# GpSimd takes three of the four products of each early rotary embedding, TensorE sums two more row tiles of the modulation, VectorE's order in the opening is set anew

## The chip, the cores and the metric

One core of a Trainium2 chip runs the whole program. The metric is the time of one execution on the device in microseconds, as the median of several runs; the kernel before takes 719.49 us (three runs, 719.28 to 719.74).

## The reference, cut to what matters

Two layers act on x, 512 rows of 1024 features. Each layer first works out a modulation from a conditioning vector c, then a gain-and-shift of the normalised rows, then a mixer, and adds the gated result to x:

```python
shift, scale, gate = split(silu(c) @ mod_w[i] + mod_b[i], 3)
h = rms_norm(x, norm_g[i]) * (1 + scale) + shift
q, k, v, g = split(h @ w_in)                 # layer 0: retention
q = rope(q, positions) * HK ** -0.5          # x1*cos - x2*sin, x1*sin + x2*cos
k = rope(k, positions)
scores = (q @ k.T) * decay                   # 4 heads, 256 wide
o = layer_norm(scores @ v)
x = x + gate * ((o * silu(g)) @ w_out)
```

Layer 1 is an attention with forget gates over 16 heads; the change does not touch it. Only the opening of layer 0 matters below: the sum over the 1024 rows of `mod_w` that gives shift and scale, the products of h with the weights of q and k, and the rotary embedding (rope) of q and k of the first two heads.

## The kernel before, in words

**Numbers.** Products are made from pairs: an operand is cut into a high part in a short format (`wh`, `act`) and the rest (`wl`, the second `act`), and TensorE adds three products (high by high, high by low, low by high). ScalarE casts the high part, VectorE subtracts it to get the low part: `wl<-raw,wh` (128x1024), `act<-x,act` and `act<-rt,act` (128x512).

**The opening.** x comes in as four row tiles of two halves. ScalarE squares them with a running sum, VectorE makes the reciprocal roots and scales the tiles, TensorE transposes them (`p<-ident,x`), ScalarE copies the result out (`big<-p`). The modulation comes in four groups of 256 columns of shift and of scale, `m0`, `m2`, `m4`, `m6`; a group is eight row tiles of `mod_w`, two in a transfer. `DIRECT` (line 38) says for each group how many of its eight row tiles TensorE sums itself, with the weights as the stationary operand and one column of `csilu` as the moving one (`r<-csilu,raw`, 128x1, four calls a row tile). The other row tiles are summed by VectorE into `macc` (one TENSOR_SCALAR, then SCALAR_TENSOR_TENSOR, each waiting for the one before), and four calls `r<-ones,macc` then sum over the partitions. In the kernel before, `m0` has four direct row tiles, the others none. After a group, VectorE writes `mod_a` and `mod_s`, ScalarE makes two feature tiles of h (`act` and `x`), VectorE the low parts, and TensorE can multiply. The first products fill six banks, `s`: q and k of head 0 and q of head 1, 18 products for each of the eight feature tiles, 144 in all. Where TensorE would have nothing to do before them, the planner puts products that nobody reads, `s<-ones_r` (here called fillers), since in the profile the granted clock of TensorE falls to 0.50 for a stretch behind one with little work.

**The ropes.** ScalarE copies the six banks to SBUF (`kept`, tiles `rt`). The function `rope` then makes four products of 128x512 with cos and sin (tiles `trig`), one difference and one sum; the results are split into high and low parts, which the score products `r<-act,act` of head 0 read. For the three ropes of the opening (q and k of head 0, q of head 1) all operands lie in SBUF; later ropes read PSUM.

**Who sets the order.** Nothing is ordered by hand. Every operation is recorded by `Sched` with a priority; `order` then runs through a model of the five engines with a cost for each operation (`cost`), and writes each engine's queue in the order in which the model started the work. On the chip each engine takes its queue strictly in that order and waits on semaphores. So a change of the model's costs moves instructions on all engines. All recorded operations carry the line of one helper, L448, in the profile. The model's costs that the change touches: a DMA's bytes, GpSimd's time for an element-wise operation, and the doubled cost of a TensorE call in a tick of 3.41 us that follows a tick with little work.

**GpSimd's queue** in this stretch holds, before the change, only DMA issues: four transfers `raw<-in_ret_w_in` that add weights onto weights in SBUF for head 0, and then two more for head 1.

Of the kernel before, what the change touches and what calls it, by code (L numbers as in the profile page):

```python
# [10 lines left out]
ALU = mybir.AluOpType  # L11
# [23 lines left out]

ORD = "m0:2 q0:0 k0:0 m2:2 q1:0 m4:2 q0:1 k0:1 m6:2 q1:1"

DIRECT = (4, 0, 0, 0)

SUMS = -22.0  # L40

# [3 lines left out]

ROPE_AT = 32

LATE_SS = 4

GO = (-20.0, -15.0, -10.0, -5.0)  # L50

LATER = 4.0

LAST = (1, 2, 3)

# [128 lines left out]
class Sched:  # L184
# [7 lines left out]
    def __init__(self, tc, kinds, phys):  # L192
        self.tc, self.kinds, self.phys = tc, kinds, phys
        self.tasks, self.clock, self.off, self.extra = [], 0.0, 0.0, []
        self.made = {k: 0 for k in kinds}
        self.uid = 0
        for attr in self.ENG:
            setattr(self, attr, Proxy(self, attr, getattr(tc.nc, attr)))

# [48 lines left out]
    def cost(self, t, op, args, kw, ins, outs):  # L248

        n = max([v.words() for v in outs], default=0)  # L250
        if op == "dma_start":
            v = (ins + outs)[0]
            t.bytes = 4 * v.words() * (v.part[1] - v.part[0])
            if not outs:
                t.bytes = 4 * ins[0].words() * (ins[0].part[1] - ins[0].part[0])
            if "accum_op" in kw:
                t.bytes *= 4
            return {"POOL": 1.02, "SP": 0.06, "ACT": 0.1}[t.eng]
        if t.eng == "PE":
            if op == "transpose":  # L260
                t.cols = 256
                return 0.109
            m = args[2].words()
            t.cols = m if args[2].dtype == F32R else 4 * m
            if m < 64:
                return 0.213
            return max(0.109, 0.002 + m / 2260.0) if args[2].dtype == F32R else max(0.109, m / 600.0)
        ptr = sum(isinstance(kw.get(k), View) for k in ("scale", "bias", "scalar", "scalar1"))
        if t.eng == "ACT":
            if op == "activation" and args[2] in TABLES:  # L270
                t.table = TABLES[args[2]]
            sb = ins[0].buf.kind not in PSUM_KINDS
            return 0.052 + n / 1200.0 + 0.093 * (ptr + ("accum_out" in kw)) + 0.042 * sb
        if t.eng == "POOL":
            return 0.1 + n / (510.0 if op == "tensor_scalar" else 450.0)
        n = max([n] + [v.words() for v in ins])
        psum = any(v.buf.kind in PSUM_KINDS for v in ins + outs)
        fast = op in ("tensor_scalar", "tensor_copy") and not psum
        return 0.069 + 0.061 * ptr + n / (1920.0 if fast else 960.0)
# [19 lines left out]
    def order(self):  # L299
# [7 lines left out]
        busy = {e: True for e in avail}  # L307
        ev, count, out, table = [(START, 0, -i, e, None) for i, e in enumerate(busy)], 0, [], None
        hw = dma = reach = 0.0
        soft, soft_wait = [], []  # L310
        ticks = {-1: 0}
        left = sum(t.eng == "PE" for t in tasks)
        for t in tasks:
# [17 lines left out]
        while True:  # L331
            moved = True
            while moved:
                moved = False
                for e in avail:
                    if busy[e]:
                        continue
                    held, got = [], None
                    while avail[e]:
                        x = heapq.heappop(avail[e])  # L340
                        if fits(x[2]):
                            got = x[2]
                            break
                        held.append(x)
                    for x in held:
                        heapq.heappush(avail[e], x)
                    if got is None and e == "PE" and now > 1.5 and self.idle is not None and self.idle.buf.slot is not None:

                        got = self.filler()
                    if got is None:  # L350
                        continue
                    moved = True
                    if self.idle is not None and e == "PE" and not got.filler and self.idle.buf in got.bufs:
                        self.idle = None
                    for b in got.new:
                        ph = self.kinds[b.kind][0]
                        b.slot = free[ph].pop(0)
                        used[b.kind] += 1
                        turn[b.kind] += 1
                    out.append(got)  # L360
                    got.start = now
                    if e == "PE":
                        tick = int(now / TICK)
                        if ticks.get(tick - 1, 0) < TICK_COLS:
                            got.cost *= 2.0
                        tick = int((now + got.cost) / TICK)
                        ticks[tick] = ticks.get(tick, 0) + got.cols
                    if e == "PE":
                        left -= not got.filler or got is self.first
                        reach = max(reach, got.prio) if left else now + 1e9  # L370
                    busy[e] = True
                    count += 1
                    end = now + got.cost
                    if got.table not in (None, table):
                        end += 1.3
                        table = got.table
                    heapq.heappush(ev, (end, 0, count, e, None))
                    if got.bytes:
                        if e == "POOL":
                            soft.append(got)  # L380
                            a = end + 0.6
                        else:
                            hw = max(hw, now + 0.05) + 0.45
                            a = hw + 0.6
                        heapq.heappush(ev, (a, 3, count, None, got))
                    else:
                        got.done = end
                        heapq.heappush(ev, (end, 1, count, None, got))
# [3 lines left out]
            while ev and ev[0][0] <= now:  # L392
                _, what, _, e, t = heapq.heappop(ev)
                if what == 0:
                    busy[e] = False
                elif what == 3 and t.eng == "POOL" and t is not soft[0]:

                    soft_wait.append(t)
                elif what == 3:
                    dma = max(now, dma) + t.bytes / 360e3  # L400
                    t.done = dma + 0.5
                    if t.eng == "POOL":
                        t.done = now + t.bytes / 360e3 + 1.4
                    count += 1
                    heapq.heappush(ev, (t.done, 1, count, None, t))
                elif what == 1:
                    if t.bytes and t.eng == "POOL":
                        soft.pop(0)
                        if soft and soft[0] in soft_wait:
                            count += 1  # L410
                            soft_wait.remove(soft[0])
                            heapq.heappush(ev, (now, 3, count, None, soft[0]))
                    for b in t.bufs:
                        b.users -= 1
                        if b.users == 0 and b.kind is not None:
                            free[self.kinds[b.kind][0]].append(b.slot)
                            used[b.kind] -= 1
                    for s in t.next:
                        lat = self.LAT if t.eng != s.eng else 0.0 if t.eng == "PE" else 0.13
                        s.ready = max(s.ready, t.done + lat)  # L420
                        s.wait -= 1
                        if not s.wait:
                            count += 1
                            heapq.heappush(ev, (s.ready, 2, count, None, s))
                else:
                    heapq.heappush(avail[t.eng], (t.prio, t.seq, t))
        if ev or any(avail.values()):
            todo = {e: [(t.emit[1], [(b.kind, b.seq) for b in t.new]) for _, _, t in sorted(avail[e])[:4]]
# [99 lines left out]
def trunk(tc, x, c, positions, mod_w, mod_b, norm_g, ret_w_in, ret_w_out, fox_w_in, fox_b_f,  # L528
# [6 lines left out]
    with ExitStack() as es:  # L535
# [348 lines left out]
        xt = []  # L884
        for t in range(NT):
            xt.append([s.buf("x", 512) for _ in range(2)])
            with s.at(-60.0):
                for hf in range(2):
                    SY.dma_start(xt[t][hf], xs[t * P:(t + 1) * P, hf * 512:hf * 512 + 512])
        with s.at(-60.0):  # L890
            pc = pr_(64)
            T.transpose(pc[:, 0:8], crow, ident[0:8, 0:8])
# [127 lines left out]
        def rope(key, b1, b2):  # L1020
            t1, t3 = (s.buf("rt") for _ in range(2))
            t2, t4 = (s.buf("rt") for _ in range(2)) if b1.buf.kind in PSUM_KINDS else (b1, b2)
            V.tensor_tensor(out=t1, in0=b1, in1=cos, op=ALU.mult)
            V.tensor_tensor(out=t3, in0=b1, in1=sin, op=ALU.mult)
            V.tensor_tensor(out=t2, in0=b2, in1=sin, op=ALU.mult)
            V.tensor_tensor(out=t4, in0=b2, in1=cos, op=ALU.mult)
            res = []
            V.tensor_tensor(out=t1, in0=t1, in1=t2, op=ALU.subtract)
            V.tensor_tensor(out=t3, in0=t3, in1=t4, op=ALU.add)
# [731 lines left out]
```

## Time and profile before

| | |
|---|---|
| median of three runs | 719.49 us (719.28 to 719.74) |
| the profiled execution | 719.05 us |
| its span, first to last instruction | 717.2 us |
| TensorE busy | 700.6 us, 98% of the span |
| VectorE busy | 603.2 us, 84% |
| GpSimd busy | 123.4 us, 17% |
| first product of the layer (`s<-act,wh`) | starts at 23.11 us |
| last stop of TensorE in the opening | ends at 68.86 us |
| first score product (`r<-act,act`) | starts at 95.75 us |

The span is read with the work around it in mind: an execution's time is about 1.9 us above its span. TensorE's busy share counts fillers too, so the opening has to be read in the timeline, not in the share. A group of the profile joins rows of the same tiles; a one-column product of 32-bit operands leaves two records for each call.

### The profile page before, as it was taken

To read this page: it belongs to the slowest core of one execution; us is meant where nothing else is said; L and a number is where in the kernel's file an instruction comes from. 1 tells how busy PE (TensorE), PEld (TensorE's weight loads), DVE (VectorE), ACT (ScalarE), POOL (GpSimd) and SP (SyncE) were. 2 spreads that over 40 slices of the span, in tenths; PEclk is the share of its full clock that TensorE was granted. 3 is DMA by queue.
4 is the path that set the end of the run, shared out by engine and by line. 5 is a ranking of instruction groups with operands and counts; after the bars stand their busy time and mean duration, and the time that the engine had idled before them with its cause. 6 is when DMAs were issued, how large, how long until landed. Compare 5 with 4: busy or idle time off the path is not lost.

```text
span 717.2 us, 10155 instructions
## 1 busy us (share of the span) xinstructions
PE 700.6 (98%) x3362; PEld 575.1 (80%) x3362; DVE 603.2 (84%) x1309; ACT 409.1 (57%) x761; POOL 123.4 (17%) x171
## 2 busy tenths in 40 slices
PE   7999999999999999999999999999999999999995
PEld 6777888888888888888888887788887788888884
DVE  5899999999969786998997979876687977799825
ACT  6558573655355435875524554547667577789512
POOL 1001100200010001002000100054352355531011
PEclk9999999999999999999999999999999999999998
DMA  8993864877666627717668118495655566736202
GB/s 283 349 323 82 186 219 112 175 234 231 129 149 208 198 37 160 273 53 146 204 198 302 74 65 286 146 220 128 162 137 135 126 165 144 177 112 186 82 17 100
DMA packets 79634, 120.34 MB, mean 168 GB/s; under 512 B 7016, under 2 KB 39904, under 8 KB 79584
## 3 DMA queue, kind: packets, MB, share of 16 engines
q1 hardware_dynamic: 66176, 98.71, 42.4%
q0 software_dynamic: 13408, 21.01, 17.1%
q8 instruction: 26, 0.43, 0.3%
q14 instruction: 24, 0.20, 0.1%
HBM read 111.25 MB, written 4.25 MB: 161 GB/s over the span
## 4 chain that ended last, share of the span: by engine, by line
PE 78%; DVE 9%; ACT 2%; issue 2%; DMA 1%; POOL 1%; DVEq 0%; POOLq 0%; ACTq 0%
PE p L448 52%; PE r L448 15%; PE a L448 11%; DVE wl L448 1%; DVE t L448 1%; DVE xn L448 1%; POOL lg L448 1%; ACT lg L448 1%; DVE sx L448 1%; DVE st L448 1%; DVE x L448 1%; DVE tg L448 1%; DMA ck<-in_k_mask 1%; DMA st<-st 0%; ACT st L448 0%
## 5 line engine op out<-in xcount | busy, mean ns | idle before, releaser
L448 DVE TENSOR_TENSOR wl<-raw,wh 128x1024 fp32r<-128x1024 f32 x126 | 153.4, 1222 | 21.9 <-ACT wh L448 11.3
L448 ACT CAST wh<-raw 128x1024 fp32r<-128x1024 f32 x126 | 131.3, 1052 | 68.5 <-PE p L448 41.6
L448 PE MATMUL p<-wh,big 128*128 128x512 f32 x384 | 135.6, 402 | 0.0
L448 PEld LDWEIGHTS p<-wh,big 128*128 128x128 f32 x384 | 71.8, 189 | 13.1
L448 PE MATMUL p<-wh,sf 128*128 128x512 f32 x256 | 80.6, 392 | 0.0
L448 PE MATMUL p<-wl,big 128*128 128x512 f32 x192 | 76.4, 398 | 0.0
L448 POOL DMA_DIRECT2D raw<-in_ret_w_in x16 | 19.4, 1212 | 257.1 <-ACT sf L448 62.4
L448 PE MATMUL p<-wh,act 128*128 128x512 f32 x192 | 62.8, 393 | 0.0
L448 DVE SCALAR_TENSOR_TENSOR macc<-raw,csilu,macc 128x512 f32<-128x512 f32 x80 | 59.6, 746 | 0.6
L448 POOL TENSOR_SCALAR lg<-lg,t 128x512 f32<-128x512 f32 (+1 forms) x64 | 42.6, 712 | 82.4 <-DVE t L448 68.2
L448 PEld LDWEIGHTS p<-wh,sf 128*128 128x128 f32 x256 | 48.0, 188 | 9.6
L448 PE MATMUL p<-act,wh 128*128 128x512 f32 x160 | 53.3, 393 | 0.0
L448 PE MATMUL p<-wl,sf 128*128 128x512 f32 x128 | 50.2, 392 | 0.0
L448 PE MATMUL p<-big,wh 128*128 128x512 f32 x128 | 46.4, 420 | 0.0
L448 PE MATMUL r<-act,sh 128*128 128x512 f32 x120 | 42.7, 391 | 0.1
L448 PEld LDWEIGHTS p<-wh,act 128*128 128x128 f32 x192 | 36.0, 188 | 7.3
L448 PEld LDWEIGHTS p<-wl,big 128*128 128x128 f32 x192 | 36.2, 189 | 6.2
L448 ACT ACTIVATE lg<-lg,t 128x512 f32<-128x512 f32 (+1 forms) x64 | 35.9, 562 | 9.1 <-DVE t L448 8.7
L448 PE MATMUL p<-wh,go 128*128 128x512 f32 x112 | 39.2, 402 | 0.2 <-DVE oa L448 0.2
L448 PE MATMUL p<-wl,act 128*128 128x512 f32 x96 | 37.8, 394 | 0.6 <-DVE wl L448 0.6
L448 POOL DMA_DIRECT2D ck<-in_k_mask x32 | 28.5, 1083 | 52.2 <-DVE t L448 52.2
L448 DVE TENSOR_TENSOR ph<-r,ph 128x128 fp32r<-128x128 f32 (+2 forms) x64 | 30.8, 485 | 6.8 <-ACT ph L448 6.3
(203 smaller groups left out, 1574.4 us busy)
## 6 DMA issues: line engine op xcount, KB each, us to landing
raw<-in_ret_w_in SPq DMA_DIRECT2D x48, 512.0 KB, 4.9
raw<-in_mod_w SPq DMA_DIRECT2D x64, 256.0 KB, 6.0
raw<-in_fox_w_in SPq DMA_DIRECT2D x32, 512.0 KB, 4.5
raw<-in_ret_w_in POOLq DMA_DIRECT2D x16, 512.0 KB, 6.3
raw<-in_mod_w SPq DMA_DIRECT2D x16, 512.0 KB, 4.7
raw<-in_ret_w_out SPq DMA_DIRECT2D x16, 512.0 KB, 4.8
ck<-cum_dram SPq DMA_DIRECT2D x16, 448.0 KB, 4.3
x<-in_x SPq DMA_DIRECT2D x16, 256.0 KB, 5.5
```

Of the source, the lines that this page charges most:

```text
L448: getattr(eng, op)(*[real(v) for v in args], **{k: real(v) for k, v in kw.items()})
```

## The change

Five edits:

- `DIRECT` goes from (4, 0, 0, 0) to (4, 2, 0, 0): the first two row tiles of `m2` are summed by TensorE. That is eight more one-column calls and one small product that puts the bias into the bank; VectorE sums six row tiles there in place of eight, and the bias is no longer added by it.
- `ROPE_E = "VGGG"`: where a rope's operands lie in SBUF, its first product stays on VectorE and the other three go to GpSimd. Three ropes, nine products.
- The model: GpSimd's element-wise operations are costed at n/340 in place of n/450, the loads of x with 1.45 times their bytes, and calls of 64 columns or fewer are not doubled in a slow tick.
- `LOOK`: in the model's first 30 us, VectorE doesn't start an operation when one of better priority will be ready within 0.2 us.
- The order of every queue in the opening follows from these.

```diff
-DIRECT = (4, 0, 0, 0)
+DIRECT = (4, 2, 0, 0)
+ROPE_E = "VGGG"
+SLOW = 1.45
+LOOK = 30.0
...
+            t.bytes *= self.slow
...
-            return 0.1 + n / (510.0 if op == "tensor_scalar" else 450.0)
+            return 0.1 + n / (510.0 if op == "tensor_scalar" else 340.0)
...
+                    if got is not None and e == "DVE" and now < LOOK and any(
+                            x.prio < got.prio - 1.0 and x.ready < now + 0.2 and fits(x) for x in soon):
+                        heapq.heappush(avail[e], (got.prio, got.seq, got))
+                        continue
...
-                        if ticks.get(tick - 1, 0) < TICK_COLS:
+                        if ticks.get(tick - 1, 0) < TICK_COLS and got.cols > 64:
                             got.cost *= 2.0
...
+            s.slow = SLOW
             with s.at(-60.0):
                 for hf in range(2):
                     SY.dma_start(xt[t][hf], xs[t * P:(t + 1) * P, hf * 512:hf * 512 + 512])
+            s.slow = 1.0
...
-            V.tensor_tensor(out=t1, in0=b1, in1=cos, op=ALU.mult)
-            V.tensor_tensor(out=t3, in0=b1, in1=sin, op=ALU.mult)
-            V.tensor_tensor(out=t2, in0=b2, in1=sin, op=ALU.mult)
-            V.tensor_tensor(out=t4, in0=b2, in1=cos, op=ALU.mult)
+            eng = [V if b1.buf.kind in PSUM_KINDS or c == "V" else G for c in ROPE_E]
+            for e, o, i0, i1 in zip(eng, (t1, t3, t2, t4), (b1, b1, b2, b2), (cos, sin, sin, cos)):
+                e.tensor_tensor(out=o, in0=i0, in1=i1, op=ALU.mult)
```

What this moves, at three places.

**TensorE ahead of the first product of the layer.** `raw_113` and `raw_116` are the direct row tiles of `m0`, `macc` the rest of `m0`, `s_119<-ones_r` the fillers, `s<-act,wh` the first products. Before:

```order
L448 MATMUL p_286<-ident,x_111 128x128 x4
L448 MATMUL r_247<-csilu,raw_113 128x1 x2
L448 MATMUL r_247<-csilu,raw_116 128x1 x8
L448 MATMUL r_247<-ones,macc_278 128x1 x4
L448 MATMUL s_119<-ones_r 128x512 x5
L448 MATMUL s_347<-act_337,wh_309 128x512
```

With the change (`raw_132` is the first transfer of `m2`):

```order
L464 MATMUL p_298<-ident,x_111 128x128 x4
L464 MATMUL r_237<-csilu,raw_116 128x1 x8
L464 MATMUL r_319<-vecs,ident 128x4
L464 MATMUL s_119<-ones_r 128x512 x2
L464 MATMUL r_237<-ones,macc_292 128x1 x4
L464 MATMUL s_119<-ones_r 128x512 x5
L464 MATMUL r_319<-csilu,raw_132 128x1 x2
L464 MATMUL s_119<-ones_r 128x512
L464 MATMUL r_319<-csilu,raw_132 128x1 x6
L464 MATMUL s_368<-act_352,wh_324 128x512
```

The sums of `m2`'s two row tiles and six fillers now stand between `m0`'s last sum and the first product, where five fillers stood. Ahead of the transposes, eleven fillers stand in place of four.

**VectorE and GpSimd at the ropes.** `rt` are rope tiles, `trig` cos and sin, `vr` and the `act` beside it the values of head 0, `wl` low parts of weights. VectorE before, from the first rope product on:

```order
L448 TENSOR_TENSOR rt_884<-rt_670,trig_722 128x512
L448 TENSOR_TENSOR rt_889<-rt_670,trig_705 128x512
L448 TENSOR_TENSOR rt_670<-rt_686,trig_705 128x512
L448 SCALAR_TENSOR_TENSOR act_902<-vr_852,t_880,act_892 128x512
L448 TENSOR_TENSOR wl_906<-raw_675,wh_850 128x1024
L448 TENSOR_TENSOR wl_915<-raw_680,wh_882 128x1024
L448 TENSOR_TENSOR wl_924<-raw_534,wh_899 128x1024
L448 TENSOR_TENSOR wl_933<-raw_548,wh_921 128x1024
L448 TENSOR_TENSOR rt_686<-rt_686,trig_722 128x512
L448 TENSOR_TENSOR rt_884<-rt_884,rt_670 128x512
```

VectorE with the change, from its one product of q's rope to the first difference of k's rope (`rt_976<-rt_976,rt_715`); `big<-p,u` is a gate tile whose first operand lies in PSUM:

```order
L464 TENSOR_TENSOR wl_933<-raw_712,wh_903 128x1024
L464 TENSOR_TENSOR wl_942<-raw_558,wh_921 128x1024
L464 TENSOR_TENSOR wl_952<-raw_582,wh_938 128x1024
L464 TENSOR_TENSOR rt_907<-rt_907,rt_691 128x512
L464 TENSOR_TENSOR rt_912<-rt_912,rt_709 128x512
L464 TENSOR_TENSOR rt_976<-rt_715,trig_754 128x512
L464 TENSOR_TENSOR act_983<-rt_907,act_972 128x512
L464 TENSOR_TENSOR big_989<-p_810,u_931 128x512
L464 TENSOR_TENSOR act_995<-rt_912,act_985 128x512
L464 TENSOR_TENSOR big_989<-p_814,u_946 128x512
L464 TENSOR_TENSOR rt_1004<-rt_725,trig_754 128x512
L464 TENSOR_TENSOR rt_976<-rt_976,rt_715 128x512
```

Ahead of these rows stand the product `rt_907<-rt_691,trig_754`, one `wl` and one `act<-vr,t,act`. GpSimd with the change:

```order
L464 DMA raw_523<-in_ret_w_in 128x2x512
L464 TENSOR_TENSOR rt_912<-rt_691,trig_739 128x512
L464 TENSOR_TENSOR rt_691<-rt_709,trig_739 128x512
L464 TENSOR_TENSOR rt_709<-rt_709,trig_754 128x512
L464 TENSOR_TENSOR rt_978<-rt_715,trig_739 128x512
L464 TENSOR_TENSOR rt_715<-rt_721,trig_739 128x512
L464 TENSOR_TENSOR rt_1008<-rt_725,trig_739 128x512
L464 TENSOR_TENSOR rt_721<-rt_721,trig_754 128x512
L464 TENSOR_TENSOR rt_725<-rt_762,trig_739 128x512
L464 TENSOR_TENSOR rt_762<-rt_762,trig_754 128x512
L464 DMA raw_1042<-in_ret_w_in 128x2x512
```

The nine products stand behind the four transfers of head 0 and ahead of the transfers of head 1; VectorE's difference `rt_907<-rt_907,rt_691` reads what the second of them writes, its sum `rt_912<-rt_912,rt_709` what the first and the third write, and `rt_976<-rt_976,rt_715` what the fifth writes.

**TensorE at the scores of head 0**, with the change. `act_972`, `act_983` are q's first half, `act_1022` and `act_1037` high and low part of k's first half:

```order
L464 MATMUL p_734<-wh_938,sf_171_816 128x512
L464 MATMUL r_1040<-act_972,act_1022 128x512
L464 MATMUL r_1040<-act_983,act_1022 128x512
L464 MATMUL r_1040<-act_972,act_1037 128x512
L464 MATMUL r_1049<-act_972,act_1022 128x384
```

The three halves of the product stand at the same place in TensorE's queue as before the change, some 300 products behind the first of the layer, and ten of them run on k's first half before thirteen products of head 1's k follow.

More of the change, by code (lines that the diff above doesn't have):

```diff
@@ L196, in __init__ @@
         self.uid = 0
+        self.slow = 1.0
         for attr in self.ENG:
@@ L309, in order @@
         hw = dma = reach = 0.0
-        soft, soft_wait = [], []
+        soft, soft_wait, soon = [], [], []
         ticks = {-1: 0}
@@ L424, in order @@
                             heapq.heappush(ev, (s.ready, 2, count, None, s))
-                else:
+                            if s.eng == "DVE":
+                                soon.append(s)
+                else:
+                    if t in soon:
+                        soon.remove(t)
                     heapq.heappush(avail[t.eng], (t.prio, t.seq, t))
```

## The prediction, made before the changed kernel was run

> **What bounds the kernel now.** I read the page's busy times first, then TensorE's waits, then the timeline of the opening.
>
> ```profile
> PE 700.6 (98%) x3362; PEld 575.1 (80%) x3362; DVE 603.2 (84%) x1309; ACT 409.1 (57%) x761; POOL 123.4 (17%) x171
> PE s L448 <- DVE act L448: 0.9, 2, 0.5
> PE s L448 <- ACT act L448: 0.6, 1, 0.6
> PE p L448 <- DVE wl L448: 0.6, 1, 0.6
> ```
>
> TensorE is the bound: 98% busy. Only what makes it stop, or run at the lower clock, moves the end. Of its waits behind the first product of the layer these four matter, 2.1 us together; the timeline places them, and columns are start, length, operation.
>
> ```profile
> 9.45 1.20 PE L448 MATMUL s<-ones_r 128*128 128x512 f32 x4
> 11.50 3.56 PE L448 MATMUL p<-ident,x 128*128 128x128 f32 x16 [0.85 <-ACT x L448]
> ...
> 16.38 1.94 PE L448 MATMUL p<-ident,x 128*128 128x128 f32 x16
> 18.16 2.29 PE L448 MATMUL r<-csilu,raw 128*128 128x1 f32 x20
> 20.31 1.03 PE L448 MATMUL r<-ones,macc 128*128 128x1 f32 x8
> 21.20 2.12 PE L448 MATMUL s<-ones_r 128*128 128x512 f32 x5
> 23.11 1.91 PE L448 MATMUL s<-act,wh 128*128 128x512 f32 x4
> ...
> 34.22 1.66 PE L448 MATMUL s<-act,wh 128*128 128x512 f32 x6 [0.62 <-ACT act L448]
> 36.27 0.50 PE L448 MATMUL s<-act,wh 128*128 128x512 f32 x1 [0.39 <-DVE act L448]
> ...
> 45.50 0.50 PE L448 MATMUL s<-act,wh 128*128 128x512 f32 x1 [0.55 <-DVE act L448]
> ...
> 68.86 0.50 PE L448 MATMUL p<-wl,act 128*128 128x512 f32 x1 [0.58 <-DVE wl L448]
> ```
>
> The four products from 23.11 take 1.91 us, 0.48 each; the six from 34.22 take 1.66, 0.28 each. The windows give the reason: a granted clock of 0.50, there and under the first transposes.
>
> ```profile
> 12.00:14.00 2.00, 2.00 (x11) 2.00 (x10) 1.80 (x15) 1.73 (x4) 0.00 (x0) 0.50 1.10 347
> 22.00:25.00 3.00, 3.00 (x9) 2.32 (x8) 2.88 (x6) 2.64 (x4) 0.00 (x0) 0.50 1.10 354
> ...
> 80.00:95.00 15.00, 15.00 (x68) 12.43 (x67) 14.93 (x22) 7.58 (x11) 1.20 (x1) 1.00 0.98 254
> ```
>
> So the opening loses the 2.1 us of waits and about 1.0 us of half clock (from 23.11 to some 25.0, at half speed): **3.1 us** is all that a better opening can give back. In the last row, TensorE and VectorE are both full from 80 to 95; that is where the ropes lie.
>
> **The opening, worked out.** Taken off VectorE are two of the eight links of `m2`'s chain of sums:
>
> ```profile
> 26.13 3.11 DVE L448 SCALAR_TENSOR_TENSOR macc<-raw,csilu,macc 128x512 f32<-128x512 f32 x4
> 32.36 0.16 DVE L448 TENSOR_TENSOR mod_a<-r,vecs 128x2 f32<-128x2 f32 x1
> ```
>
> A link is 0.67 to 0.79 us, so 1.3 to 1.6, and its order no longer drops other work between them. `m2` is what the waits at 34.22 and 36.27 hang on (`mod_a` is written at 32.36), `m4` the one at 45.50, a group behind on the same engine. All three, 1.6 us, should go.
>
> TensorE pays. Its ten calls at 18.16 take 2.29 us, 0.23 each; eight more are 1.83, the bias product some 0.1. They stand ahead of the first product and so delay it unless TensorE was free. I follow the queue: eleven fillers at 0.25 to 0.30 from 9.45 end near 12.2, and the transposes start 0.7 us later than at 11.50; if the fillers hold the clock up, the first 16 transposes take 1.94 us as the second 16 do, and not 3.56 (1.6 less); two fillers and the bias add 0.6. `m0`'s last sum, which ended at 21.3, ends at 21.3 + 0.7 - 1.6 + 0.6 = 21.0. Then six fillers (1.5) and eight calls (1.8): the first product at 24.3 in place of 23.11, **1.2 us later**. The half clock (1.0) should be gone, since more fillers lie in the stretch. The wait at 68.86 stays (VectorE is 1.3 us earlier, TensorE about as much): say 0.3 of it is left over and above. Sum: 1.6 + 1.0 - 1.2 + 0.2 = 1.6 us gained. Bounds: 3.1 us gained at best; at worst the clock is at 0.50 over the eight calls (1.8 more) and one further stretch of products (3.4 us at half speed, 1.7), 2 us lost. I take **-1.6**.
>
> The remaining edits (costs of x's loads and of GpSimd, small calls, `LOOK`) touch no duration; they act by the order that this sum follows.
>
> **The ropes, worked out.** Off VectorE come nine products of 0.60 us from start to start, 5.4 us in all. On GpSimd the operation exists in the trace only at the end:
>
> ```profile
> 691.66 1.29 POOL L448 TENSOR_TENSOR x<-x,x 128x512 f32<-128x512 f32 x1 [39.81 <-ACT tm L448]
> 696.82 0.75 DVE L448 SCALAR_TENSOR_TENSOR x<-x,t,x 128x512 f32<-128x512 f32 x1
> 697.10 1.61 POOL L448 TENSOR_TENSOR x<-x,x 128x512 f32<-128x512 f32 x1 [4.15 <-ACT tm L448]
> ```
>
> 1.29 us alone, 1.61 where it overlaps the last 0.47 us of a VectorE operation with two inputs in SBUF. Rows from the attention say more:
>
> ```profile
> 497.00 1.89 POOL L448 TENSOR_SCALAR lg<-lg,t 128x256 f32<-128x256 f32 x2 [0.97 <-DVE t L448]
> 497.51 1.23 DVE L448 TENSOR_TENSOR wl<-raw,wh 128x1024 fp32r<-128x1024 f32 x1 [0.60 <-ACT wh L448]
> 507.13 0.83 POOL L448 TENSOR_SCALAR lg<-lg,t 128x256 f32<-128x256 f32 x2 [1.95 <-DVE t L448]
> L448 DVE TENSOR_TENSOR qn<-qn,t x16: 676/684/941, 437.8 to 565.0; 128x512 f32<-128x512 f32 x16
> 558.38 1.78 POOL L448 TENSOR_SCALAR lg<-lg,t 128x256 f32<-128x256 f32 x2 [0.85 <-DVE t L448]
> 558.46 1.54 DVE L448 TENSOR_TENSOR qn<-qn,t 128x512 f32<-128x512 f32 x2
> ```
>
> The same pair of GpSimd operations takes 0.83 us in the clear and 1.89 with one `wl<-raw,wh` of 1.23 beside it: 1.06 more, nearly that operation's whole length. At 558 GpSimd was at work when VectorE began, and VectorE's operation took 0.94 in place of 0.68 (the longest of 16). I read this as one way to SBUF that either holds while the other waits, and VectorE's next operation in line keeps it. [...]
>
> What does VectorE run beside the nine products? Its groups from 79.7 to 98.1 (busy, mean):
>
> ```profile
> L448 DVE TENSOR_TENSOR wl<-raw,wh 128x1024 fp32r<-128x1024 f32 x6 | 7.2, 1222 | 0.0
> L448 DVE TENSOR_TENSOR rt<-rt,trig 128x512 f32<-128x512 f32 x8 | 5.4, 687 | 0.0
> L448 DVE TENSOR_TENSOR act<-rt,act 128x512 fp32r<-128x512 f32 x4 | 2.7, 687 | 0.0
> L448 DVE TENSOR_TENSOR rt<-rt,rt 128x512 f32<-128x512 f32 x4 | 2.6, 686 | 0.0
> L448 DVE SCALAR_TENSOR_TENSOR act<-vr,t,act 128x512 fp32r<-128x512 f32 x2 | 1.5, 748 | 0.0
> L448 DVE TENSOR_TENSOR big<-p,u 128x512 f32<-128x512 f32 x2 | 1.4, 686 | 0.0
> ...
> 80.49 2.01 DVE L448 TENSOR_TENSOR rt<-rt,trig 128x512 f32<-128x512 f32 x3
> 83.08 4.78 DVE L448 TENSOR_TENSOR wl<-raw,wh 128x1024 fp32r<-128x1024 f32 x4
> 97.33 0.69 DVE L448 TENSOR_TENSOR act<-rt,act 128x512 fp32r<-128x512 f32 x1
> 95.75 3.26 PE L448 MATMUL r<-act,act 128*128 128x512 f32 x15
> ```
>
> No idle time, and only `big` reads PSUM: the rest, 19.4 of the 21 us, has two SBUF inputs. Let T0 be the start of VectorE's first rope product (80.49 before; some 1.3 earlier now). With the new order and full lock-out: product 0.60, `act` 0.66 and four `wl` at 1.18 lead to T0+6.0 with nothing done on GpSimd. The first difference needs its second product: T0+8.6. The sum needs the third, T0+9.9, and ends at 10.5. Six operations of 0.60 follow, to 14.1; GpSimd has the 1.2 us of the two `big` for its fourth and fifth product and needs 2.6: k's first difference starts at T0+15.5. It, two sums, a `wl` and the `act` take 3.5: k's low part stands at **T0+19.0**. Without lock-out no wait remains, and it is T0+14.3.
>
> TensorE came to the scores at 95.75, T0+15.3 then. With the opening's 1.6 us gained and VectorE's 1.3, it comes 0.3 nearer, to T0+15.0, and its third score product, 0.5 later, reads k's low part: a wait of 19.0 - 15.5 = 3.5 us. k's second half needs GpSimd's seventh product (two more, 2.6 us, with no free time beside VectorE's row): T0+21.6, and four operations later, T0+24.0, its low part stands; TensorE, released at 19.0, has eight score products (1.3), thirteen others (2.95) and two more before it, and waits 0.3. Together 3.8. Where GpSimd holds the way when VectorE wants it, VectorE waits too: 0.26 in the row of `qn`, at most 1.29 for a product. At three or four such meetings that is 1 to 4 us; I take 1.2, near the row. The rope term: **+5.0**, from 0 (all hidden; there is no gain, since TensorE doesn't stop at the scores now) to 8 (3.8 + 4). The third rope's products end the row on GpSimd and are needed a head later. Behind them on GpSimd's queue stand head 1's transfers, the first of which was issued here before:
>
> ```profile
> 120.85 1.20 POOL L448 DMA_DIRECT2D raw<-in_ret_w_in  x1 [39.51 <-DVE t L448]
> ```
>
> GpSimd had been idle for 39.5 us, so products that end near 106 delay nothing there.
>
> Sum on the profiled execution, 719.05: -1.6 + 5.0 = **+3.4, 722.45**. It lies 0.44 under the median of the runs, 719.49, so for the median I say **722.9**.
>
> **The rivals.**
>
> *Hidden products (faster).* GpSimd's fifth product must be done by about T0+12 for TensorE not to stop; begun at T0 that is 2.4 us a product at most. If the way is shared finely, or VectorE's own waits for casts leave it free often enough, a product takes 1.3 to 2.4 us, and only the opening is left: 719.49 - 1.6 = 717.9, at best 716.4. For it: the 1.61 us with a partial overlap; against it, 1.06 us of lock-out by one `wl`, and a VectorE without a gap. 0.24.
>
> *Half lock-out (the same).* GpSimd slips in at the seams, and VectorE is never held: half of 3.8, 1.9, against 1.6: 719.8. 0.14.
>
> *A cold clock on top (slower).* Eight one-column calls ahead of the first product are little work, as 18.2 to 21.2 was, behind which the clock fell to 0.50 at 22. If the clock is down there again, the opening loses 2 in place of gaining 1.6, and with the ropes the time is 719.49 + 2 + 5 = 726.5. Against it: six fillers now stand among the calls. [...] 0.14.
>
> **How the numbers follow.** My forecast, lock-out with a warm opening, 0.48. An interval of 0.2% is about what a measurement of this kernel can tell from no change, 718.05 to 720.93. Faster: the hidden case's 0.24 less a little, 0.23. The same: 0.15. Slower: forecast and cold clock, 0.62. The range 717.2 to 727.2 takes in the hidden case, the forecast with its bounds (719.5 to 726) and most of the cold one; the forecast's own range is 720.5 to 726.
>
> **What would show it.** GpSimd's rows `rt<-rt,trig` between 78 and 106 us: 2.5 us or more on average is lock-out, 1.3 to 2.0 is not. VectorE idle before `rt<-rt,rt`, put down to GpSimd, and TensorE idle before `r<-act,act` of 3 us or more, put down to VectorE's or ScalarE's `act`. In the opening: no wait at 34, 36 and 45 us, the first product near 24.3 us, a granted clock of 1.00 from 12 to 25. I am wrong if TensorE doesn't stop at the scores, or if the opening itself is slower.

## The result, and the profile after

The changed kernel takes 729.38 us (median of four runs, 728.02 to 729.80), the kernel before 719.62 beside it: a ratio of 1.0133, with a 95% interval of 1.0115 to 1.0150. By that ratio it is 9.6 us slower, where 3.4 had been forecast, and above the range of 717.2 to 727.2. The profiled execution has a span of 726.9 us, against 717.2.

First the page of the changed kernel (busy times) and TensorE's waits (total, times, longest):

```profile
PE 705.9 (97%) x3391; PEld 579.6 (80%) x3391; DVE 606.3 (83%) x1297; ACT 408.8 (56%) x761; POOL 138.3 (19%) x180
PE r L464 <- DVE act L464: 3.4, 1, 3.4
PE r L464 <- ACT act L464: 3.3, 1, 3.3
PE p L464 <- DVE wl L464: 1.7, 3, 0.9
```

Nine products have left VectorE, yet it is busy 3.1 us longer than the 603.2 before. TensorE has two waits of over 3 us, and the timeline puts both at the scores of head 0:

```profile
24.44 1.40 PE L464 MATMUL s<-act,wh 128*128 128x512 f32 x5
...
83.85 0.50 PE L464 MATMUL p<-wl,sf 128*128 128x512 f32 x1 [0.57 <-DVE wl L464]
...
87.78 0.50 PE L464 MATMUL p<-wl,sf 128*128 128x512 f32 x1 [0.92 <-DVE wl L464]
...
99.27 0.73 PE L464 MATMUL r<-act,act 128*128 128x512 f32 x2 [3.26 <-ACT act L464]
103.44 2.50 PE L464 MATMUL r<-act,act 128*128 128x512 f32 x8 [3.43 <-DVE act L464]
```

The windows of the changed kernel give the clock (columns: stretch, length, busy time and count on PE, PEld, DVE, ACT and POOL, granted clock, DMA share, GB/s):

```profile
12.00:25.00 13.00, 13.00 (x106) 12.38 (x106) 9.92 (x28) 9.54 (x15) 0.00 (x0) 1.00 1.10 349
...
95.00:101.00 6.00, 1.74 (x7) 0.81 (x5) 5.96 (x6) 1.86 (x3) 5.92 (x4) 1.00 0.99 322
101.00:108.00 7.00, 4.57 (x14) 3.99 (x15) 7.00 (x11) 3.93 (x6) 0.10 (x1) 0.52 0.01 2
```

The opening runs at full clock; behind the two waits the clock is at half, and 4.57 us of work at 0.52 is 2.2 us lost.

To see where time is gained and lost I matched the two traces by the columns that TensorE has worked off (fillers and one-column products left out; the times are those of the kernel before). At 80 us the changed kernel is 2.0 us **ahead**. At 90 it is 0.1 behind: the two waits for `wl`, 1.5 us, and about 0.6 at their edges (the first product behind each takes 0.50 us in place of 0.39). At 105 it is 9.2 behind: 3.26 + 3.43 of waits and the 2.2 of half clock. Near 560 another 0.5 is lost, and the end is 9.7 late. So the opening did what was forecast, and between 83 and 108 us of the changed kernel, 11.2 us were lost.

The timeline of VectorE of the changed kernel in that stretch (columns: start, length, operation):

```profile
79.90 2.77 DVE L464 TENSOR_TENSOR rt<-rt,trig 128x512 f32<-128x512 f32 x1
82.58 1.21 DVE L464 TENSOR_TENSOR wl<-raw,wh 128x1024 fp32r<-128x1024 f32 x1
83.72 1.77 DVE L464 SCALAR_TENSOR_TENSOR act<-vr,t,act 128x512 fp32r<-128x512 f32 x1
85.42 5.68 DVE L464 TENSOR_TENSOR wl<-raw,wh 128x1024 fp32r<-128x1024 f32 x3
91.02 1.28 DVE L464 TENSOR_TENSOR rt<-rt,rt 128x512 f32<-128x512 f32 x2
...
93.43 0.68 DVE L464 TENSOR_TENSOR big<-p,u 128x512 f32<-128x512 f32 x1
94.03 1.18 DVE L464 TENSOR_TENSOR act<-rt,act 128x512 fp32r<-128x512 f32 x1
95.13 0.68 DVE L464 TENSOR_TENSOR big<-p,u 128x512 f32<-128x512 f32 x1
95.73 1.17 DVE L464 TENSOR_TENSOR rt<-rt,trig 128x512 f32<-128x512 f32 x1
96.82 1.74 DVE L464 TENSOR_TENSOR rt<-rt,rt 128x512 f32<-128x512 f32 x1
98.49 1.49 DVE L464 TENSOR_SCALAR macc<-raw,csilu 128x512 f32<-128x512 f32 x1
100.01 1.63 DVE L464 SCALAR_TENSOR_TENSOR macc<-raw,csilu,macc 128x512 f32<-128x512 f32 x1
...
102.70 0.68 DVE L464 TENSOR_TENSOR act<-rt,act 128x512 fp32r<-128x512 f32 x1
```

And GpSimd's, with the idle time before a row and what ended it in brackets:

```profile
80.31 1.80 POOL L464 TENSOR_TENSOR rt<-rt,trig 128x512 f32<-128x512 f32 x1
82.81 6.07 POOL L464 TENSOR_TENSOR rt<-rt,trig 128x512 f32<-128x512 f32 x3 [0.70 <-DVE rt L464]
93.05 8.05 POOL L464 TENSOR_TENSOR rt<-rt,trig 128x512 f32<-128x512 f32 x5 [4.17 <-DVE rt L464]
125.50 2.44 POOL L464 DMA_DIRECT2D raw<-in_ret_w_in  x2 [24.41 <-DVE raw L464]
```

Read the durations against what the same operations take in the kernel before, from 78 to 112 us, with no product of GpSimd beside them: 0.69 for a product, 1.22 for a `wl`, 0.75 for `act<-vr,t,act`, 0.48 for the first link of a chain. Where GpSimd works, VectorE's operations are longer by 2.1, 1.0, 2.1 (over three `wl`), 0.5, 0.5, 1.1, 1.0 and 0.9 us: **9.1 us held for nine products**. From 88.9 to 93.05, when GpSimd has nothing to do, they are as short as ever; and the two `big<-p,u`, whose first operand lies in PSUM, are not held at all though GpSimd works right through them. GpSimd's products take 1.77 us on average, not 2.5, and VectorE has no idle time in this stretch that ends with a result of GpSimd: it is held, it does not wait for results. The shares are uneven, and the first is the largest: 2.1 us for one product of GpSimd beside it.

### The profile page after: what moved, and what is told of

The parts are those of the page before. It is cut to its first block, busy times and chain, and to the rows that moved or that the text cites. A ratio compares the mean times of both kernels' runs of the same rounds, so it can differ in the third digit from the quotient of the medians.

```text
span 726.9 us, 10219 instructions
## 1 busy us (share of the span) xinstructions
PE 705.9 (97%) x3391; PEld 579.6 (80%) x3391; DVE 606.3 (83%) x1297; ACT 408.8 (56%) x761; POOL 138.3 (19%) x180
## 4 chain that ended last, share of the span: by engine, by line
PE 77%; DVE 8%; ACT 1%; issue 1%; DVEq 0%; ACTq 0%
PE p L464 50%; PE r L464 17%; PE a L464 11%; DVE wl L464 1%; DVE t L464 1%; DVE xn L464 1%; ACT st L464 1%; DVE rt L464 1%; DVE st L464 1%; DVE x L464 1%; DVE big L464 1%; DVE act L464 0%; ACT lg L464 0%; DVE oa L464 0%; DVE go L464 0%
## 5 line engine op out<-in xcount | busy, mean ns | idle before, releaser
L464 DVE TENSOR_TENSOR wl<-raw,wh 128x1024 fp32r<-128x1024 f32 x126 | 155.8, 1241 | 24.2 <-ACT wh L464 10.9
```

The costliest lines, as they stand in the source:

```text
L464: getattr(eng, op)(*[real(v) for v in args], **{k: real(v) for k, v in kw.items()})
```

## The experiments

Ratios are against runs of the kernel before on the same chip (medians 719.3 to 720.0 us).

| kernel | median, us | ratio, 95% interval |
|---|---|---|
| the change | 729.4 | 1.0133 [1.0115, 1.0150] |
| its opening alone | 719.5 | 0.9998 [0.9984, 1.0011] |
| its order, products on VectorE | 725.3 | 1.0068 [1.0054, 1.0083] |
| its ropes alone | 730.8 | 1.0146 [1.0133, 1.0159] |
| before, nine spare products added | 730.6 | 1.0146 [1.0133, 1.0160] |
| the same, half as wide | 724.5 | 1.0070 [1.0057, 1.0083] |
| the same, one input | 725.2 | 1.0083 [1.0070, 1.0096] |
| the change, TensorE kept at work | 726.8 | 1.0103 [1.0090, 1.0116] |
| opening alone, angles on ScalarE | 719.4 | 1.0000 [0.9992, 1.0009] |
| opening alone, ropes sooner | 720.8 | 1.0019 [1.0004, 1.0034] |
| the change, ropes sooner | 730.5 | 1.0167 [1.0139, 1.0195] |

### Who holds whom: spare products beside the order of before

The theory after reading the two traces: GpSimd and VectorE take turns at SBUF, one instruction each, so VectorE pays for each product whether or not anything depends on it. The test adds nine products that nobody reads; the rest keeps the order of the kernel before. The edit, shortened:

```diff
-V.tensor_tensor(out=t3, in0=b1, in1=sin, op=ALU.mult)        # and the two after it
+t = V.tensor_tensor(out=t3, in0=b1, in1=sin, op=ALU.mult)
+t.spare = (spare[:, 0:512], cos[:, 0:512], sin[:, 0:512])    # issued behind t:
+gpsimd.tensor_tensor(out=spare, in0=cos, in1=sin, op=ALU.mult)
```

> The kernel before in its own order, with all twelve rope products on VectorE, and nine products of the same size added on GpSimd that read the two trigonometric tiles and write a tile that nobody reads then; nothing waits for them. Theory A (GpSimd and VectorE take turns at SBUF, one instruction each, whatever depends on them): VectorE is held 9 times about 1.0 us between 81 and 97 us, k's parts come 8 to 9 us later, TensorE waits as long at the scores and its clock falls behind it: 727 to 731. Rival B (VectorE waited for GpSimd's results, not for its access): 719 to 720, with VectorE's operations at 0.68 and 1.22 us as before. Rival C (VectorE keeps the access, as forecast, and GpSimd is what stretches): 719 to 721, GpSimd's products at 2.5 us or more.

It took 730.6 us, 1.5% more: as much as the ropes alone. In its trace GpSimd, the four `wl` behind the products, and TensorE's first wait:

```profile
81.41 17.40 POOL L451 TENSOR_TENSOR gate<-trig,trig 128x512 f32<-128x512 f32 x9
88.74 8.93 DVE L448 TENSOR_TENSOR wl<-raw,wh 128x1024 fp32r<-128x1024 f32 x4
91.07 0.80 PE L448 MATMUL p<-wl,sf 128*128 128x512 f32 x1 [5.29 <-DVE wl L448]
```

The same four `wl` took 4.78 us in the kernel before (the row at 83.08 that the prediction quotes), so each is held (8.93 - 4.78) / 4 = 1.04 us. From its first product to the `big<-p,u` VectorE's row takes 25.4 us in place of 15.0, 10.4 more: nine turns of 1.04 and about 1.0 over. The extra lies in the first product, which takes 2.74 us here as in the ropes alone (2.77 in the change); why it is held twice as long stays open. No result of GpSimd is waited for here: dependence is ruled out as the cause, and so is the forecast's picture, in which VectorE runs on and GpSimd stretches.

The two variants change one thing each: the width (256 columns), and the number of inputs (`tensor_scalar`, one tile times a constant).

> As the nine spare products on GpSimd beside the order of the kernel before, but each 256 columns wide and not 512. There, VectorE's operations beside a product became 1.0 to 1.1 us longer and the time rose by 10.7 us. Theory A (VectorE is held as long as GpSimd's instruction works, so the hold goes with its size): 0.5 to 0.6 us each, 4.5 to 5.5 in all, and 724 to 726.5 us. Rival B (a change of turns has a fixed price of 1 us): 729 to 731. Rival C (a short instruction slips in at the seams): 719.5 to 721.

> Nine spare instructions on GpSimd at the same place, 512 columns each, but TENSOR_SCALAR: one tile read, times a constant. Alone such a row takes 0.71 us on average in the kernel before (lg<-lg,t), where a product took 1.29. Theory A (any GpSimd instruction takes its turn, for the time that it works): VectorE is held 0.5 to 0.6 us each, 723 to 726 us. Rival B (only GpSimd's instructions with two inputs collide): 719.5 to 720.5, VectorE's operations at 0.68 and 1.22 as before.

Their four `wl`, half width first, then one input:

```profile
86.02 6.77 DVE L448 TENSOR_TENSOR wl<-raw,wh 128x1024 fp32r<-128x1024 f32 x4
```

```profile
84.39 5.91 DVE L448 TENSOR_TENSOR wl<-raw,wh 128x1024 fp32r<-128x1024 f32 x4
...
93.49 1.09 DVE L448 TENSOR_TENSOR act<-rt,act 128x512 fp32r<-128x512 f32 x1
```

(6.77 - 4.78) / 4 = 0.50 us each at half the width: the hold goes with the size, and apart from the first a turn has no fixed price to speak of. With one input it is 0.41, read from the `act` that takes 1.09 in place of 0.68; (5.91 - 4.78) spread over four is less, since the first of the four, at 1.21 us, was not held. So one input costs less than half of what two cost, and an instruction with one input holds VectorE too; the 0.41 is a little under the 0.5 to 0.6 expected. The times, 0.7% and 0.8% more, lie where the first theory had them. They don't follow the hold alone: VectorE's row grows by 5.5 us at half the width and by 4.0 with one input, yet the second is not faster. In its profiled execution TensorE's clock is at half for 3.4 us behind a stop of 3.2 us at the scores; at half the width the stops of 2.6 and 2.4 us have none behind them.

### The parts of the change, apart

```diff
-ROPE_E = "VGGG"
+ROPE_E = "VVVV"
```

> All edits of the change except the rope products, which stay on VectorE (the work is planned anew with that). Theory A (the ropes cost all of it; in the profile of the change TensorE stands 2.0 us ahead of the kernel before at 75 to 85 us, and the ropes come behind that): 717 to 718 us, 1.5 to 2.5 us faster than before, no wait of TensorE behind the first product above 1 us in all, and a granted clock of 1.00 from 12 to 30 us. Rival B (the planner's edits also spoil the order behind the opening): 720 us or more. Rival C (the 2.0 us are taken back by a wait further on, as the change's waits on wl and qn): 719 to 720.

Here the forecast was wrong a second time; what came is rival C, with its wait further on. In the profiled execution (span 716.6, the fastest of twelve runs) TensorE is 2.7 us ahead from 75 to 92 us, as hoped, but the median is that of the kernel before. TensorE's row at the scores and VectorE's load on the way there say why (the same columns as above):

```profile
94.43 1.90 PE L464 MATMUL r<-act,act 128*128 128x512 f32 x9 [1.18 <-ACT act L464]
...
50.00:75.00 25.00, 24.78 (x109) 20.11 (x109) 25.00 (x47) 17.65 (x27) 2.50 (x2) 1.00 0.56 144
75.00:95.00 20.00, 18.82 (x84) 15.26 (x82) 19.93 (x30) 11.54 (x18) 2.40 (x2) 1.00 0.83 214
```

VectorE has no idle time from 50 to 95 us. TensorE comes sooner and waits for k's first part; 1.2 us of the lead go there, 0.2 by 150 us and 0.5 near 560. What is left, 0.6 us in this execution, is not seen in the median; the interval, 0.9984 to 1.0011, would still allow it. Two of the twelve runs took 722.6 and 723.9 us at a mean granted clock of 0.991 and 0.990, where the ten others had 0.996 to 0.997: these two are read further down.

The change's own order, with the nine products issued on VectorE at the same places:

```diff
+t.emit = (s.tc.nc.vector,) + t.emit[1:]      # for each product planned on GpSimd
```

> The change's own order, instruction for instruction, but the nine products are issued on VectorE at the places where GpSimd had them. Nothing is held any more, and VectorE has 5.4 us of products more. Theory A (VectorE is held by GpSimd's products, 9.2 us by the rows of the change: 2.77 for 0.69, 1.77 for 0.76 and so on): VectorE's row from 79.9 us to k's first low part adds up to 18.8 us in place of 23.5, so TensorE waits some 4 us at the scores in place of 6.7, the clock may stay up, and the time is 721 to 723.5. Rival B (the order, with sums of m's chain ahead of k's low part, costs all of it): 728 to 730. Rival C (only GpSimd's lateness counted, the order is harmless): 717 to 718.

725.3: above the 721 to 723.5 expected, below the change by 0.65%, 4.7 us. VectorE's row (19.0 us) and TensorE's waits (4.3) came as expected; the clock, which was to stay up, fell to half behind them (0.65 on average from 102 to 106 us). So moving the products to GpSimd is worth +4.7 us by itself (9.1 held against 5.4 saved is 3.7; behind it TensorE's clock is at half for 6.8 us in the change and for 3.4 here), and the **order** costs the other 4.9: the opening alone, with the same products on VectorE and an order planned for that, loses nothing. The planner's model charges VectorE nothing for GpSimd's work. VectorE between k's first difference and k's first low part, and the two waits of TensorE that come of it (the profiled execution took 727.99 us, 2.7 above the median; its opening ran at half clock for 10 us, as the last section shows):

```profile
98.06 0.69 DVE L464 TENSOR_TENSOR rt<-rt,rt 128x512 f32<-128x512 f32 x1
98.66 0.49 DVE L464 TENSOR_SCALAR macc<-raw,csilu 128x512 f32<-128x512 f32 x1
99.18 0.75 DVE L464 SCALAR_TENSOR_TENSOR macc<-raw,csilu,macc 128x512 f32<-128x512 f32 x1
99.85 0.69 DVE L464 TENSOR_TENSOR rt<-rt,trig 128x512 f32<-128x512 f32 x1
100.45 1.22 DVE L464 TENSOR_TENSOR wl<-raw,wh 128x1024 fp32r<-128x1024 f32 x1
...
102.19 0.69 DVE L464 TENSOR_TENSOR act<-rt,act 128x512 fp32r<-128x512 f32 x1
...
99.45 0.74 PE L464 MATMUL r<-act,act 128*128 128x512 f32 x2 [1.60 <-ACT act L464]
102.93 2.28 PE L464 MATMUL r<-act,act 128*128 128x512 f32 x8 [2.74 <-DVE act L464]
```

Ropes alone, on the kernel before (shortened):

```diff
-V.tensor_tensor(out=t3, in0=b1, in1=sin, op=ALU.mult)     # and t2, t4
+E.tensor_tensor(out=t3, in0=b1, in1=sin, op=ALU.mult)     # E: GpSimd for b1 in SBUF
```

> The kernel before with one edit: three of the four products of each early rope on GpSimd (planned anew with the old cost of GpSimd's products). Theory A (nine products hold VectorE about 1.0 us each, and that alone makes TensorE wait at the scores): 727 to 731, with VectorE's operations beside a product 0.9 to 1.1 us longer. Rival B (the loss needs the change's opening or its planner): 719 to 723.

730.8, at the upper end of what the first theory allowed. With another order the loss sits in another place, and is as large. Here dependence has a share: VectorE stands idle 1.16 us for a result of GpSimd, at 100 us. TensorE's longest wait, 6.94 us for `big` behind the scores, in its timeline:

```profile
104.42 0.77 PE L448 MATMUL p<-wh,act 128*128 128x512 f32 x1 [6.94 <-DVE big L448]
```

### The half clock behind the waits

The change with more work for TensorE in its two waits (shortened):

```diff
+t.ahead = [(q_high, q_high)] * 12 + [(k_high, q_high)] * 13   # TensorE, ahead of the first score product,
+                                                              # into its own bank and overwritten by it
```

> The change itself, and 25 more products of 512 columns on TensorE ahead of the first score product, into its own bank and overwritten by it: 12 on q's parts, which stand long before, and 13 on k's first part, so that they run in the two waits of 3.26 and 3.43 us. Theory A (the half clock behind the waits, from 101 to 108 us, costs 2.3 us by itself): granted clock 1.00 from 95 to 110, TensorE idle there under 1.5 us in all in place of 6.7, and 726.5 to 727.8 us. Rival B (VectorE sets the pace there anyway, and TensorE at half speed loses nothing): 729 to 730. Rival C (the extra products are in the way): 730 or more.

TensorE's timeline of this kernel (the first two rows are the added products), and the window that was at 0.52:

```profile
95.31 2.88 PE L465 MATMUL r<-act 128*128 128x512 f32 x12
98.77 3.24 PE L465 MATMUL r<-act,act 128*128 128x512 f32 x13 [0.58 <-ACT act L466]
...
102.98 1.44 PE L466 MATMUL r<-act,act 128*128 128x512 f32 x8 [0.51 <-DVE act L466]
...
101.00:108.00 7.00, 6.49 (x32) 5.20 (x31) 7.00 (x11) 4.39 (x6) 0.00 (x0) 1.00 0.00 0
```

The clock stays at 1.00, the eight score products take 1.44 us in place of 2.50, and the time falls by 0.30%, 2.2 us: the price read off the windows. Work that is thrown away paid for itself against the change; the kernel before is still 1% faster.

### Can it be mended?

Two tries to bring VectorE's row to the scores sooner, with all products on VectorE; the first gives two operations on the angles to ScalarE, the second sets the ropes ahead in the planner's order (`KEEP, LATE = -4.0, 4.0` to `-4.0, -6.0`):

```diff
-V.tensor_copy(ang, pos)
-V.tensor_scalar(out=ang, in0=ang, scalar1=inv, scalar2=None, op0=ALU.mult)
+A.activation(ang, pos, AF.Copy, scale=inv)
```

> The opening's edits with all rope products on VectorE (in the profile: TensorE 2.66 us ahead of the kernel before at 75 to 95 us, and 1.4 of it lost in a wait for k's first part), and two of VectorE's operations on the angles (0.42 and 0.48 us, at 53 us) done by one of ScalarE's instead. VectorE has no idle time from 25 to 98 us, so its ropes come 0.9 us earlier. Theory A (VectorE's row up to the ropes is now the bound): the wait at the scores falls from 1.2 to some 0.3 us and the time to 718.3 to 719.0. Rival B (the wait is ScalarE's, whose casts stand in the queue): no change against the opening alone, 719.3 to 719.8.

> The opening's edits with all products on VectorE, and the ropes sooner in the order (LATE -6.0 in place of 4.0): VectorE does the first rope's second product ahead of a wl, and two big<-p,u behind the ropes. Theory A (in the opening alone TensorE comes 2.7 us sooner to the scores and gives 1.4 of it back to VectorE's row, which stands first): k's first difference 0.6 to 1.2 us sooner, 718.3 to 719.2 us. Rival B (the wl that the ropes pass are late in their turn, and TensorE waits for those): 719.5 to 721.

Neither beats the kernel before: 719.4, no difference, and 720.8, a little slower. In the first the time is rival B's, but not for its reason: the wait at the scores is gone. TensorE's waits show the stall only moved, from the scores to a `wl` at 67 us in the one and at 91 us in the other:

```profile
67.41 0.50 PE L464 MATMUL p<-wl,act 128*128 128x512 f32 x1 [0.87 <-DVE wl L464]
```

```profile
90.93 0.50 PE L464 MATMUL p<-wl,sf 128*128 128x512 f32 x1 [1.81 <-DVE wl L464]
```

The last try is the change itself with its ropes sooner (`LATE` 0.0), so that less stands between k's difference and its low part:

> The change, with the ropes' place in the planner's order four units sooner (LATE 0.0 in place of 4.0). Of what stood between k's first difference and its low part on VectorE (two sums of m's chain of 1.5 and 1.6 us, a wl of 1.2), one sum is left, so k's low part comes some 2.5 us sooner. Theory A (VectorE's time up to k's low part is what TensorE waits for, whoever holds VectorE): the second wait at the scores falls from 3.4 to about 1 us, 726 to 727.5 us, still slower than before since VectorE is held 9 us all the same. Rival B (GpSimd's products set the pace): 729 to 730.

730.5 us, no better than the change. In the profiled execution, the slowest of four at 735.73 us (its opening too ran at half clock), the waits at the scores are gone from TensorE's timeline, and these stand in their place:

```profile
100.31 0.66 PE L464 MATMUL p<-wl,sf 128*128 128x512 f32 x1 [2.20 <-DVE wl L464]
108.83 0.76 PE L464 MATMUL p<-wh,act 128*128 128x512 f32 x1 [4.13 <-DVE big L464]
```

I had expected 726 to 727.5, and the rival 729 to 730 for another reason. What the four orders have in common is VectorE with next to no gap (0.2 us at most from 75 to 95 us): whichever of its results is put last, TensorE waits for that one.

## Why the prediction was right or wrong, point by point

**TensorE is the bound.** Right over the span, and not enough for the stretch that mattered. VectorE is full as well from 50 us on, which the prediction said only of 80 to 95. There are two bounds side by side there, and a gain on one stops at the other.

**The opening, -1.6.** Right on its own ground: 2.0 us ahead at 80 us, the waits at 34, 36 and 45 gone, the first product at 24.44 (forecast 24.3), the clock at 1.00 from 12 to 25, the wait at 68.86 down to 0.24. Wrong as a term of the total: taken alone, the opening's edits change nothing that the runs can tell (0.9998). The step that failed is that the lead was carried to the end; in that kernel VectorE's ropes came 1.3 us earlier, as forecast (79.23), but k's first part was late for a TensorE that had come 2.7 earlier. In the change itself the ropes began only 0.6 us earlier (79.90).

**The ropes, +5.0.** That the two exclude each other was right (1.04 us of VectorE for a product of GpSimd that nobody reads), and the side that pays was wrong. The step that failed is "VectorE's next operation in line keeps it". The two take turns; so the 1.2 us for "VectorE waits too" was 9.1, and GpSimd's lateness, on which the ledger was built, was smaller than forecast. VectorE's own row slipped instead: first difference at T0 + 11.1 (8.6 forecast), k's first difference at T0 + 16.9 (15.5), k's low part at T0 + 23.5 (19.0), and the waits at the scores 6.7 in place of 3.8, with 1.5 for `wl` that I had not counted. GpSimd's 4.17 us of idle time before its fifth product is the same thing once more: that product overwrites the tile that VectorE's first product of k reads, and VectorE came to it at 92.22 only. The row at 497 us had misled me: there GpSimd's second instruction met one `wl` with nothing behind it, so GpSimd was seen to wait and VectorE not. That row shows who came second, not who goes first in a queue of both.

In the terms of the sum: the opening gave 2.0 (1.6 forecast), the stretch of the ropes cost 11.2 (5.0), and 0.5 near 560 had no term: 9.7 in place of 3.4. That the products on GpSimd cost 4.7 us by themselves, near the forecast 5.0, is chance: the 5.0 was put together mostly of waits for GpSimd's results, and VectorE had none.

Who is held can be read from the rows of the change and of the spare products. VectorE's instructions with two SBUF inputs are, by 1.04 us a turn (0.50 at half the width, 0.41 with one input on GpSimd); so is the first link of a chain, which reads one tile of 128x512 (`macc<-raw,csilu`, 1.49 us in place of 0.48). The two `big<-p,u`, whose first operand lies in PSUM, are not (0.68 with GpSimd at work). The sum had counted their 1.2 us as free for GpSimd, for which the prediction shows no row of the kernel before; in the change GpSimd worked through both, and neither became longer.

**The cold clock** was among the rivals at 0.14, with its place in the opening. It came, but behind the waits at the scores, where no step had looked for it: 2.2 us, and the reason why 6.7 us of waits cost 9. The waits that the prediction forecast should have carried a term for it. The length of a stop alone doesn't tell whether half clock follows: one of 1.81 us (the opening alone with the ropes sooner) and one of 2.26 (spare products; fifteen score products in 4.49 us, in place of 3.26 before) had 3.4 us of half clock behind them, those of 2.6 and 2.4 (half as wide) none. In the opening, where the rival had put it, the cold clock came as well in two other kernels with the same opening (the last section).

**The hidden products.** This rival's condition, a product of 2.4 us at most, was met by the average (1.77), and the time was lost all the same. It asked only whether GpSimd is in time.

**The signs that I had named.** Two of the three for the ropes would have misled: GpSimd at 1.3 to 2.0 us was to mean "no lock-out", and VectorE was to stand idle. A held operation shows no idle time, it shows as *busy* and long (1.77 us for `act<-vr,t,act` in the change); the sign is its duration against the same operation elsewhere (0.75 before). That TensorE would stop at the scores by 3 us or more for `act` was right, and that head 1's transfers would lose nothing behind the products was right too (issued at 125.50, after 24.41 us of idle time).

The range failed because its upper bound, 8 us for the ropes, let four meetings at most hold VectorE, and had nothing for the clock; there were nine, one for each product.

## What to carry to other kernels

Before giving GpSimd part of a full VectorE's work, charge VectorE for it: here a product of 512 columns saved VectorE 0.60 us and held it 1.04, so the move lost before any dependence was looked at. From these traces I would expect it to pay only where VectorE idles or reads PSUM; no run here tries that. When a planner orders the work, a cost that its model leaves out also spoils the order (4.9 of 9.6 us here). And when one engine is sped up, ask in the same stretch which other engine has no idle time, and allow for a lower clock behind a stop of TensorE: here 3.4 us at half came behind single stops of 1.81, 2.26 and 3.2 us, and none behind two of 2.6 and 2.4.

## What the runs showed of the hardware that was not expected

- A GpSimd instruction holds VectorE for less than the profile shows it to take alone: 1.04 us of 1.29 for a product of 512 columns (GpSimd's spans are rough in the profile: in the change its first product begins at 80.31, while the DMA issue ahead of it lasts to 80.77). The hold goes with columns and with inputs (0.50 at 256 columns, 0.41 with one input).
- The same instructions of the opening ran at two clocks. In the change the fillers and one-column sums ahead of the first product kept it at 1.00; with the same instructions in the same order, the profiled execution of the change's order on VectorE shows this:

```profile
20.42 1.74 PE L464 MATMUL s<-ones_r 128*128 128x512 f32 x5
...
23.24 2.55 PE L464 MATMUL r<-csilu,raw 128*128 128x1 f32 x12
25.66 2.48 PE L464 MATMUL s<-act,wh 128*128 128x512 f32 x5
...
24.00:28.00 4.00, 4.00 (x15) 3.52 (x15) 3.69 (x6) 0.00 (x0) 0.00 (x0) 0.50 1.11 349
```

  Five products that take 1.40 us in the change take 2.48, and TensorE is 3.9 us later at 75 us than in the change. The change with its ropes sooner, whose opening is the same again, ran it at half clock from 22 to 32 us in the execution of 735.73 us (its five products take 2.48 us as well). That the two runs of the opening alone at 722.6 and 723.9 us are of this kind fits their clock, but they were not profiled. What decides between the two clocks was not shown.
- The 0.5 us lost near 560 us is a wait of TensorE of 0.4 us for `qn` (0.39 at 569.11 in the change). It came also with spare products and the order of before, and did not come with spare products half as wide. What decides it stays open.
